# A third raw weight buffer, low parts on VectorE in the gated unit, and token scaling inside the transposing product

## The chip, the core and the metric

The kernel runs on one NeuronCore of a Trainium2 chip. Five engines work side by side, each through its own queue in order: TensorE (PE in the profile: matrix products; PEld is its weight load), VectorE (DVE), ScalarE (ACT), GpSimd (POOL) and SyncE (SP), which here only issues DMAs. GpSimd issues DMAs too, the accumulating ones of this kernel. SBUF is the on-chip memory of 128 partitions; PSUM holds TensorE's results, in 8 banks of 128 x 512 float32. The metric is the device time of one execution in microseconds.

## What is computed

One decoder block, batch 1, 512 tokens of width 1024 with 16 meta tokens put in front (528 in all), float32 throughout:

```python
h = jnp.concatenate([meta, x], axis=1)
n = _rmsnorm(h, g_mix[layer])
proj = n @ w_in[layer]                       # 1024 -> z 1024 | xbc 1536 | dt 16 | u 1024
xbc = jax.nn.silu(_causal_depthwise_conv(proj[..., o_xbc:o_dt], conv_w[layer], conv_b[layer]))
y_ssd = _ssd_mixer(xbc, dt_raw, z, ...)      # Mamba-2, 16 heads of 64, state 128
y_s5 = _s5_mixer(u, ...)                     # 64 groups, complex diagonal scan, then the gated unit
mix = jnp.concatenate([y_ssd, y_s5], axis=-1)
h = h + mix @ w_out[layer]
m = _rmsnorm(h, g_mlp[layer]) @ w_up[layer]
h = h + jnp.square(jax.nn.relu(m)) @ w_down[layer]
return _rmsnorm(h, g_final)[:, N_META:]
```

The gated unit at the end of the S5 branch is `v = gelu(y) @ w_glu + b_glu`, 1024 by 2048, and `v[:, :1024] * sigmoid(v[:, 1024:])`, normed.

## The kernel before

**Split products.** TensorE multiplies in a reduced float32 (F32R), so each operand is split into a high part (a cast) and a low part (what the cast lost), and each product is three: high with high, high with low, low with high. Tokens are kept transposed (width on the partitions), as `xhi` and `xlo`. A weight tile of 128 x 8 x 128 values (512 KB) goes through three rings in the pool `wp`: `load_weight` (L102) loads it into `raw` (2 buffers) from SyncE's queue, and `split_weight` (L108) makes `whi` and `wlo` (3 buffers each). There are two ways for the low part. With `lo_engine=V` ScalarE casts the high part (L116) and VectorE subtracts it from the raw tile (L117). Otherwise ScalarE writes minus the rounded tile into `wlo` (L120), a DMA from GpSimd's queue adds the raw tile to it (L121), and ScalarE casts the high part (L122). The raw buffer is free when its last reader is done, in the second way the DMA. Loads and splits are given a lead (`AHEAD`, 3000 instructions) in the planner's order.

**Order.** The program is written in the order of the block, but a planner, which simulates the engines with its own instruction times, sets the order on each queue: the ready instruction with the highest priority goes next, so that xbc and z tiles fill the gaps of S5, and gated tiles those of the SSD chunks. At run time each queue keeps that order and waits with semaphores.

**Stages, in the order of time.** (1) Norm and transposition: `norm_transpose_split` (L164) for the meta tokens and four tiles of 128 tokens. `rstd_of` (L145) squares on ScalarE (L148) and takes the power on GpSimd (L151); VectorE multiplies the tile by the factor (L166); TensorE transposes it in eight 128 x 128 pieces against `ident` (L170); VectorE multiplies by the gain (L172), ScalarE casts the high part (L175), VectorE subtracts (L176). (2) Eight u tiles (`u_split` L244, `u_half` L249), 24 products each per half of the tokens, copied to `ut` and to DRAM (`Ud`). Tiles 0 and 1 are loaded between the tokens; tile 2 has VectorE's low part, the other seven GpSimd's. GpSimd clears the tables `WB`, `CC`, `Tp` and two `decay` buffers behind the last power (L478 to L480). (3) Eight S5 blocks (`s5_block` L489): small products, VectorE scans over `decay` (L572), round trips through DRAM (`Kd` to `Tp`, `Ud` to `ub`, `Yd`), with 12 xbc and 8 z tiles as filling, all by GpSimd's way. (4) The gated unit (L875 to L898), 16 weight tiles by GpSimd's way, filling the SSD chunks (L724): there `ab`, the decay rows of eight heads, is read from DRAM by SyncE (L749), masked by GpSimd (L752), exponentiated by ScalarE (L756) and multiplied on VectorE (L758). ScalarE's copy `btok` (L798) feeds the state product `pst` (L801). `sg` and `y5` of the gated unit (L882, L886) have two buffers each. (5) The output product (`rows_product` L818): S5 half first (VectorE's low parts), then the SSD half in two column halves, the first of four slabs with GpSimd's low parts (L934), the second with VectorE's. (6) The MLP in four quarters: `up_tile` (L953) and `block_product` (L1050), a seven-product scheme whose sums `S1`, `S2`, `S3` are tiles made by `Sums.new` (L1025).

Of the kernel before, what the change touches and what calls it, by code (L numbers as in the profile page):

```python
# [10 lines left out]
F32 = mybir.dt.float32  # L11
# [3 lines left out]
ALU = mybir.AluOpType  # L15
# [3 lines left out]
P = 128  # L19
SEQ = 512  # L20
# [3 lines left out]
DM = 1024  # L24
# [7 lines left out]
TS5 = 4  # L32
NC5 = L // TS5
# [5 lines left out]
AHEAD = 3000  # L39
# [6 lines left out]
def bc(ap, axis, n):  # L46
    a = ap.unsqueeze(axis)
    shape = list(a.shape)
    shape[axis] = n
    return a.broadcast_to(shape)  # L50
# [3 lines left out]
def hybrid_block_kernel(ctx, tc, x, meta_tokens, g_mix, w_in, conv_w, conv_b, dt_bias, a_log, d_ssd,  # L54
                        g_ssd, lam_re, lam_im, log_step, b_re, b_im, c_re, c_im, d_s5, w_glu, b_glu,
                        g_s5, w_out, g_mlp, w_up, w_down, g_final, out, dbg=None):
    nc = tc.nc
    V, A, G, T = nc.vector, nc.scalar, nc.gpsimd, nc.tensor
# [42 lines left out]

    def load_weight(src, a, b, ahead=AHEAD):  # L102
        with (tc.high_priority(offset=ahead) if ahead else nullcontext()):
            raw = wp.tile([P, a, b], F32, tag="raw", name="raw", bufs=2)
            dma(out=raw, in_=src)
        return raw

    def split_weight(raw, lo_engine=None, ahead=AHEAD, room=None):  # L108
        with (tc.high_priority(offset=ahead) if ahead else nullcontext()):
            if room is None:  # L110
                hi = wp.tile(list(raw.shape), F32R, tag="hi", name="whi", bufs=3)
                lo = wp.tile(list(raw.shape), F32R, tag="lo", name="wlo", bufs=3)
            else:
                hi, lo = room("whi", list(raw.shape)), room("wlo", list(raw.shape))
            if lo_engine is V:
                A.copy(hi, raw)  # L116
                V.tensor_tensor(out=lo, in0=raw, in1=hi.bitcast(F32), op=ALU.subtract)  # L117
            else:

                A.mul(lo, raw, -1.0)  # L120
                G.dma_start(out=lo.bitcast(F32), in_=raw, accum_op=ALU.add)  # L121
                A.copy(hi, raw)  # L122
        return hi, lo
# [4 lines left out]
    def w_cols(w, c0, n=P, lo_engine=None):  # L128
        return split_weight(load_cols(w, c0, n), lo_engine)
# [15 lines left out]
    def rstd_of(src, n, name):  # L145
        junk = scr[:, 3]
        v = mid.tile([P, 1], F32, tag="ssq", name="ssq")
        A.activation(out=junk[:n], in_=src, func=AF.Square, accum_out=v[:n])  # L148
        V.tensor_scalar(out=v[:n], in0=v[:n], scalar1=1.0 / DM, scalar2=EPS, op0=ALU.mult, op1=ALU.add)
        r = mid.tile([P, 1], F32, tag="rstd", name=name)  # L150
        last_pow.append(G.tensor_tensor(out=r[:n], in0=v[:n], in1=mhalf[:n, 0:1], op=ALU.pow))  # L151
        return r
# [9 lines left out]
            V.tensor_tensor(out=xlo[:, 4 * h:4 * h + 4, c0:c0 + n], in0=src_p, in1=hi.bitcast(F32), op=ALU.subtract)  # L162

    def norm_transpose_split(src, n, gcol, xhi, xlo, c0):  # L164
        r = rstd_of(src, n, "rstd")
        last_xn.append(V.tensor_scalar(out=src, in0=src, scalar1=r[:n, 0:1], scalar2=None, op0=ALU.mult))  # L166
        for h in range(2):
            pt = bank("pt")
            for k in range(4):
                T.transpose(pt[:, k * n:(k + 1) * n], src[:, (4 * h + k) * P:(4 * h + k + 1) * P], ident[:n, :n])  # L170
            xg = xgs[:, next(turn) % 3, 0:4 * n].rearrange("p (k n) -> p k n", k=4)
            V.tensor_tensor(out=xg, in0=pt[:, 0:4 * n].rearrange("p (k n) -> p k n", k=4),  # L172
                            in1=bc(gcol[:, 4 * h:4 * h + 4], 2, n), op=ALU.mult)
            hi = xhi[:, 4 * h:4 * h + 4, c0:c0 + n]
            A.copy(hi, xg)  # L175
            V.tensor_tensor(out=xlo[:, 4 * h:4 * h + 4, c0:c0 + n], in0=xg, in1=hi.bitcast(F32), op=ALU.subtract)  # L176

    s5_ctx = tc.tile_pool(name="s5", bufs=1)
    s5 = s5_ctx.__enter__()
    scr = slot("scr", [P, 4, DM])  # L180
    mt = scr[0:NM, 2]
    xgs = scr[:, 0:2].rearrange("p a (h c) -> p (a h) c", h=2)
    turn = itertools.count()
    last_pow, last_xn = [], []
    xt = slot("xt", [P, 4, DM])
    xhi = slot("xhi", [P, KD, L], F32R)
# [56 lines left out]

    def u_split(f):  # L244
        raw = first_raw[f] if f in first_raw else load_cols(w_in[0], O_U + f * P)
        uw[f] = split_weight(raw, V if f == 2 else G, 0 if f < 3 else AHEAD)
        uts[f] = s5.tile([P, TS5, NC5], F32, tag="ut", name="ut", bufs=2)

    def u_half(f, i):  # L249
# [222 lines left out]
    NB = 2  # L472
# [1 line left out]
    CC = [s5.tile([P, 2, 4, 5, 2, 16], F32, name=f"CC{i}") for i in range(NB)]  # L474
    Tp = [s5.tile([P, 4, P], F32, name=f"Tp{i}") for i in range(NB)]

    decay = [s5.tile([P, 4, NC5], F32, name=f"decay{i}") for i in range(NB)]
    with tc.issue_after(last_pow[-1].ins):  # L478
        for t in (WB, *CC, *Tp, *decay):
            G.memset(t, 0.0)  # L480
    Kd = [dr.tile([P, P], F32, name=f"Kd{f}") for f in range(8)]

# [6 lines left out]
    def s5_block(b):  # L489
# [65 lines left out]
        for hf in range(2):  # L555
# [10 lines left out]
            V.tensor_tensor(out=wi[:, jj], in0=px[1], in1=co[:, jj], op=ALU.mult)  # L566
            V.tensor_tensor(out=tw[:, jj], in0=px[0], in1=si[:, jj], op=ALU.mult)
            V.tensor_tensor(out=wi[:, jj], in0=wi[:, jj], in1=tw[:, jj], op=ALU.subtract)
        A.copy(decay[i][:, :, 1:], bc(r4[:, js], 2, NC5 - 1))
        for w in (wr, wi):  # L570
            w = w.rearrange("p j c -> p (j c)")
            V.tensor_tensor_scan(out=w, data0=decay[i].rearrange("p j c -> p (j c)"), data1=w, initial=0.0,  # L572
                                 op0=ALU.mult, op1=ALU.add)
        sr = s5.tile([P, 4, NC5], F32, tag="sr", name="sr", bufs=1)
        si_ = s5.tile([P, 4, NC5], F32, tag="si", name="si", bufs=1)
# [297 lines left out]
    sqa = sd.tile([P, SEQ], F32, tag="sqa", name="sqa", bufs=1)  # L873
    yy = (yghi, yglo)
    for f in range(8):  # L875
        wv = w_cols(w_glu[0], f * P)
        pv = bank("pv")
        mm_cols(pv, wv, yy, P, slice(0, SEQ))
        wg = w_cols(w_glu[0], DM + f * P)
        pg = bank("pg")  # L880
        mm_cols(pg, wg, yy, P, slice(0, SEQ))
        sg = sd.tile([P, SEQ], F32, tag="sg", name="sg")  # L882
        A.activation(out=sg, in_=pg, func=AF.Tanh, scale=0.5, bias=hbg[:, 8 + f:9 + f])
        hv = mid.tile([P, SEQ], F32, tag="acc", name="hv")
        A.activation(out=hv, in_=pv, func=AF.Identity, scale=0.5, bias=hbg[:, f:f + 1])
        y5 = sd.tile([P, P, TS5], F32, tag="y5", name="y5")  # L886
        V.scalar_tensor_tensor(out=y5.rearrange("p c t -> p t c"), in0=sg.rearrange("p (t c) -> p t c", t=TS5),
                               scalar=1.0, in1=hv.rearrange("p (t c) -> p t c", t=TS5), op0=ALU.add, op1=ALU.mult)
        y5f = y5.rearrange("p c t -> p (c t)")
        if f == 0:  # L890
            dump("y50", y5f)
            A.activation(out=sqa, in_=y5f, func=AF.Square)
        else:
            A.activation(out=sg, in_=y5f, func=AF.Square)
            vadd(sqa, sqa, sg)
        A.activation(out=y5hi[:, f], in_=y5f, func=AF.Copy, scale=col("gs5", f))
        V.scalar_tensor_tensor(out=y5lo[:, f], in0=y5f, scalar=col("gs5", f), in1=y5hi[:, f].bitcast(F32),
                               op0=ALU.mult, op1=ALU.subtract)  # L898
# [32 lines left out]
        transpose_split(xs[:, t], P, hhi, hlo, t * P)  # L931

    ylist = [(yhi[:, k], ylo[k // 2][:, k % 2]) for k in range(KD)]
    rows_product(ylist, w_out[0], 0, 4, 0, G, mix_first)  # L934
    spares = [slot2(name, [P, 3, 2, 512], F32R) for name in ("spareh", "sparel")]
    spare = iter([t[:, n] for n in range(3) for t in spares])

# [80 lines left out]
    class Sums:  # L1018
# [4 lines left out]
            self.s = {}  # L1023

        def new(self, m):  # L1025
            self.s[m] = ml.tile([P, 2, HT], F32, tag=m, name=m, bufs=1 if m == "S3" else 2)
            return self.s[m]

        def get(self, m):
# [126 lines left out]
```

## Time and profile before

| | |
|---|---|
| median of 3 runs | 848.06 us (844.64 to 848.61) |
| profiled execution | 852.09 us, of which 850.4 us from its first to its last instruction |
| mean granted TensorE clock | 0.973 |
| weight tiles with GpSimd's low part / VectorE's | 47 / 42 |
| bytes moved by DMA | 116.28 MB, 24.64 MB of it on GpSimd's queue |
| GpSimd's 47 low-part DMAs, median from issue to landing | 5.3 us |

A row of groups gives the line, the engine, the operation, what is written and read, the count, busy us and mean ns, then the idle time before and what ended it. A row of waits gives the waiting engine and line, what it waited for, total us, times and the longest. A row of stages gives the stretch, each engine's busy us with its count, the granted clock, the DMA share and GB/s. A row of the chain of work or of a timeline starts with start and duration in us.

### The profile page before, as it was taken

How to read it: one execution, taken by the hardware profiler on the slowest of the kernel's cores; microseconds unless marked ns; L12 is line 12 of the kernel's file. 1: busy time of each engine (PE TensorE's matmuls, PEld its weight loads, DVE VectorE, ACT ScalarE, POOL GpSimd, SP SyncE). 2: the span in 40 equal slices, each digit the busy share in tenths (PEclk: the TensorE clock that was granted, in tenths of full speed). 3: DMA queues.
4: the chain of work that ended last, by engine and by line, in shares of the span. 5: the costliest groups of instructions: out<-in, count | busy, mean ns of one | idle time of the engine just before them, and what ended most of it. 6: DMA issues, size and time to landing. Idle time of an engine off the chain costs nothing.

```text
span 850.4 us, 11626 instructions
## 1 busy us (share of the span) xinstructions
PE 794.7 (93%) x4351; PEld 669.5 (79%) x4351; DVE 585.0 (69%) x961; ACT 449.8 (53%) x711; POOL 66.9 (8%) x115
## 2 busy tenths in 40 slices
PE   5998799899899599879999999999999999999996
PEld 4898799898787387667888888888888888888875
DVE  6873789989765456556731557688848885887395
ACT  7575589788655646536513344345334533543254
POOL 5110001011000111111001010000000000000001
PEclk9999999999999889998999999999999999999998
DMA  9988665667677588776626636434133423331002
GB/s 220 187 202 187 151 151 121 157 151 175 163 156 200 124 184 187 162 167 153 235 74 151 176 111 208 124 99 149 55 94 105 143 75 94 104 124 49 1 2 99
DMA packets 144865, 116.28 MB, mean 137 GB/s; under 512 B 22092, under 2 KB 122616, under 8 KB 144808
## 3 DMA queue, kind: packets, MB, share of 16 engines
q1 hardware_dynamic: 138040, 90.89, 37.6%
q0 software_dynamic: 6768, 24.64, 15.5%
q8 instruction: 34, 0.56, 0.3%
q14 instruction: 23, 0.19, 0.1%
HBM read 83.93 MB, written 6.95 MB: 107 GB/s over the span
## 4 chain that ended last, share of the span: by engine, by line
PE 66%; DMA 15%; ACT 6%; DVE 4%; issue 4%; SPq 4%; POOL 0%; POOLq 0%; ACTq 0%; DVEq 0%
PE pm L138 21%; PE acc L1067 16%; PE acc L824 8%; DMA wlo<-raw 5%; PE pg L138 4%; DMA ab<-aD 3%; PE pv L138 3%; PE pxb L138 3%; PE acct L824 3%; PE acct L1067 3%; PE pz L138 2%; DMA raw<-in_w_in_dram 2%; DMA Tp<-Kd 1%; ACT wlo L120 1%; DMA Ud<-ut 1%
## 5 line engine op out<-in xcount | busy, mean ns | idle before, releaser
L138 PE MATMUL pm<-hhi,wlo 128*128 128x512 f32 (+1 forms) x272 | 104.1, 383 | 0.0
L138 PE MATMUL pm<-hhi,whi 128*128 128x512 f32 (+1 forms) x272 | 103.5, 382 | 0.0
L138 PE MATMUL pm<-hlo,whi 128*128 128x512 f32 (+1 forms) x272 | 102.6, 378 | 0.0
L117 DVE TENSOR_TENSOR wlo<-raw,whi 128x1024 fp32r<-128x1024 f32 x42 | 51.4, 1223 | 65.7 <-ACT whi L116 65.6
L116 ACT CAST whi<-raw 128x1024 fp32r<-128x1024 f32 x42 | 44.1, 1050 | 92.1 <-PE pm L138 59.8
L122 ACT CAST whi<-raw 128x1024 fp32r<-128x1024 f32 x47 | 49.1, 1044 | 62.6 <-DMA raw<-in_w_in_dram 19.9
L1067 PE MATMUL acc<-bh,al 128*128 128x512 f32 x192 | 75.7, 394 | 0.1
L1067 PE MATMUL acc<-bl,ah 128*128 128x512 f32 x192 | 75.7, 394 | 0.0
L1067 PE MATMUL acc<-bh,ah 128*128 128x512 f32 x192 | 69.9, 394 | 1.4 <-ACT ah L971 1.4
L121 POOL DMA_DIRECT2D wlo<-raw x47 | 40.6, 864 | 304.7 <-ACT wlo L120 135.2
L971 ACT CAST bh<-quad 128x1024 fp32r<-128x1024 f32 x32 | 33.7, 1054 | 49.5 <-PE acc L1067 42.4
L138 PEld LDWEIGHTS pm<-hlo,whi 128*128 128x128 f32 x272 | 51.1, 188 | 11.2
L138 PEld LDWEIGHTS pm<-hhi,wlo 128*128 128x128 f32 x272 | 51.0, 188 | 10.9
L138 PEld LDWEIGHTS pm<-hhi,whi 128*128 128x128 f32 x272 | 50.9, 188 | 10.0
L138 PE MATMUL pxb<-xhi,whi 128*128 128x264 f32 x192 | 56.6, 295 | 0.4 <-ACT xcr L686 0.4
L138 PE MATMUL pxb<-xhi,wlo 128*128 128x264 f32 x192 | 56.5, 294 | 0.0
L138 PE MATMUL pxb<-xlo,whi 128*128 128x264 f32 x192 | 56.2, 293 | 0.0
L966 DVE TENSOR_TENSOR bl<-quad,bh 128x1024 fp32r<-128x1024 f32 x32 | 39.1, 1223 | 18.6 <-ACT bh L971 18.6
L120 ACT ACTIVATE wlo<-raw 128x1024 fp32r<-128x1024 f32 x47 | 49.6, 1056 | 4.1 <-DMA raw<-in_w_glu_dram 3.9
L971 ACT CAST bh<-quads 128x1024 fp32r<-128x1024 f32 x24 | 25.2, 1051 | 41.5 <-PE acc L1067 23.3
L1067 PEld LDWEIGHTS acc<-bh,ah 128*128 128x128 f32 x192 | 36.0, 188 | 9.7 <-ACT ah L971 2.1
L1067 PEld LDWEIGHTS acc<-bh,al 128*128 128x128 f32 x192 | 36.6, 191 | 8.5 <-DVE al L966 0.5
(382 smaller groups left out, 2067.2 us busy)
## 6 DMA issues: line engine op xcount, KB each, us to landing
wlo<-raw POOLq DMA_DIRECT2D x47, 512.0 KB, 5.3
raw<-in_w_up_dram SPq DMA_DIRECT2D x32, 512.0 KB, 4.0
raw<-in_w_in_dram SPq DMA_DIRECT2D x28, 512.0 KB, 4.3
raw<-in_w_glu_dram SPq DMA_DIRECT2D x16, 512.0 KB, 4.5
raw<-in_w_out_dram SPq DMA_DIRECT2D x16, 512.0 KB, 3.4
quad<-in_w_down_dram SPq DMA_DIRECT2D x16, 512.0 KB
quads<-in_w_down_dram SPq DMA_DIRECT2D x16, 512.0 KB, 5.4
ab<-aD SPq DMA_DIRECT2D x8, 512.0 KB, 10.9
```

The source lines that it names most:

```text
L116: A.copy(hi, raw)
L117: V.tensor_tensor(out=lo, in0=raw, in1=hi.bitcast(F32), op=ALU.subtract)
L120: A.mul(lo, raw, -1.0)
L121: G.dma_start(out=lo.bitcast(F32), in_=raw, accum_op=ALU.add)
L122: A.copy(hi, raw)
L138: T.matmul(ps_out, lhsT=w[a][:, k, 0:m], rhs=x[b][:, k, tok], start=(n == 0), stop=(n == len(steps) - 1))
L824: T.matmul(acc[t], lhsT=lhs[2 * sl + k][a][:, t * P:(t + 1) * P], rhs=wt[b][:, k], start=(sl == 0 and k == 0 and n == 0), stop=(sl == n_sl ...
L966: V.tensor_tensor(out=out, in0=a, in1=b, op=ALU.subtract)
L971: A.copy(hi, src)
L1067: T.matmul(banks[bk][s], lhsT=as_[g][x][:, j, s * P:(s + 1) * P], rhs=bs[g][y][:, j], start=(first and g == 0 and j == 0 and i == 0), stop ...
```

## The change

Six edits. `raw` gets a third buffer. The low parts of the 16 gated tiles, of u tile 0 and of the four slabs of L934 move from GpSimd's DMA to VectorE's subtraction: then 26 tiles have GpSimd's low part and 63 VectorE's. The token tile is no longer multiplied by its factor; ScalarE writes the factor on a diagonal (`ident` times the factor, one of three places in the scratch tile), and the transposing product takes that diagonal as its moving operand, so it scales and transposes at once. `decay`, `sg` and `y5` lose their second buffer, and `S3` uses the buffers of `S1`.

```diff
     def load_weight(src, a, b, ahead=AHEAD):
...
-            raw = wp.tile([P, a, b], F32, tag="raw", name="raw", bufs=2)
+            raw = wp.tile([P, a, b], F32, tag="raw", name="raw", bufs=3)
...
     def norm_transpose_split(src, n, gcol, xhi, xlo, c0):
         r = rstd_of(src, n, "rstd")
-        last_xn.append(V.tensor_scalar(out=src, in0=src, scalar1=r[:n, 0:1], scalar2=None, op0=ALU.mult))
+        m = next(turn) % 3
+        diag = scr[:, 1, 640 + m * P:640 + (m + 1) * P]
+        last_xn.append(A.mul(diag[:n, :n], ident[:n, :n], r[:n, 0:1]))
         for h in range(2):
             pt = bank("pt")
             for k in range(4):
-                T.transpose(pt[:, k * n:(k + 1) * n], src[:, (4 * h + k) * P:(4 * h + k + 1) * P], ident[:n, :n])
-            xg = xgs[:, next(turn) % 3, 0:4 * n].rearrange("p (k n) -> p k n", k=4)
+                T.matmul(pt[:, k * n:(k + 1) * n], lhsT=src[:, (4 * h + k) * P:(4 * h + k + 1) * P], rhs=diag[:n, :n])
+            xg = xgs[:, next(xturn) % 3, 0:4 * n].rearrange("p (k n) -> p k n", k=4)
...
-    turn = itertools.count()
+    turn, xturn = itertools.count(), itertools.count()
...
-        uw[f] = split_weight(raw, V if f == 2 else G, 0 if f < 3 else AHEAD)
+        uw[f] = split_weight(raw, V if f in (0, 2) else G, 0 if f < 3 else AHEAD)
...
-    decay = [s5.tile([P, 4, NC5], F32, name=f"decay{i}") for i in range(NB)]
+    decay = s5.tile([P, 4, NC5], F32, name="decay")
     with tc.issue_after(last_pow[-1].ins):
-        for t in (WB, *CC, *Tp, *decay):
+        for t in (WB, *CC, *Tp, decay):
             G.memset(t, 0.0)
...
-        wv = w_cols(w_glu[0], f * P)
+        wv = w_cols(w_glu[0], f * P, lo_engine=V)
...
-        wg = w_cols(w_glu[0], DM + f * P)
+        wg = w_cols(w_glu[0], DM + f * P, lo_engine=V)
...
-        sg = sd.tile([P, SEQ], F32, tag="sg", name="sg")
+        sg = sd.tile([P, SEQ], F32, tag="sg", name="sg", bufs=1)
...
-        y5 = sd.tile([P, P, TS5], F32, tag="y5", name="y5")
+        y5 = sd.tile([P, P, TS5], F32, tag="y5", name="y5", bufs=1)
...
-    rows_product(ylist, w_out[0], 0, 4, 0, G, mix_first)
+    rows_product(ylist, w_out[0], 0, 4, 0, V, mix_first)
...
-            self.s[m] = ml.tile([P, 2, HT], F32, tag=m, name=m, bufs=1 if m == "S3" else 2)
+            self.s[m] = ml.tile([P, 2, HT], F32, tag="S1" if m == "S3" else m, name=m, bufs=2)
```

## What was predicted before the result was known

> **What bounds the kernel now.** I read the busy shares first, then the same figures by stage, then the waits of each stage.
>
> ```profile
> PE 794.7 (93%) x4351; PEld 669.5 (79%) x4351; DVE 585.0 (69%) x961; ACT 449.8 (53%) x711; POOL 66.9 (8%) x115
> ```
>
> ```profile
> core 0: us, PE busy (x) PEld busy (x) DVE busy (x) ACT busy (x) POOL busy (x), PEclk, DMA share, GB/s
> 0.00:30.00 30.00, 17.91 (x103) 15.99 (x104) 21.18 (x42) 18.25 (x36) 11.99 (x51) 0.89 0.98 215
> 30.00:80.00 50.00, 47.32 (x375) 46.70 (x374) 32.72 (x109) 35.50 (x65) 6.10 (x8) 0.97 0.79 186
> 80.00:265.00 185.00, 172.58 (x1308) 157.96 (x1307) 153.61 (x294) 135.18 (x215) 17.00 (x20) 0.98 0.68 155
> 265.00:413.00 148.00, 128.79 (x660) 99.11 (x659) 81.92 (x145) 80.98 (x152) 20.96 (x22) 0.93 0.73 171
> 413.00:825.00 412.00, 412.00 (x1855) 337.60 (x1853) 279.25 (x346) 166.97 (x222) 7.75 (x10) 1.00 0.36 108
> ```
>
> TensorE works 794.7 of 850.4 us, so all there is to win is 56 us of idle time and some lost clock. The stages say where: 12.1 us idle before 30, 2.7 to 80 (the u tiles), 12.4 to 265 (S5 with the xbc and z tiles), 19.2 from 265 to 413 (the gated unit with the SSD chunks), nothing from 413 to 825, where TensorE is busy 412.00 of 412.00 us, and the rest, 9.3, in the tail, which the change doesn't touch. In the gated stage the wait views, of TensorE, SyncE's queue and GpSimd, name the cause:
>
> ```profile
> PE pg L138 <- DMA wlo<-raw: 8.0, 1, 8.0
> PE pst L801 <- ACT btok L798: 5.9, 1, 5.9
> PE pcb L751 <- DVE S L808: 3.6, 1, 3.6
> ```
>
> ```profile
> SPq L105 <- DMA wlo<-raw: 79.9, 12, 12.9
> ```
>
> ```profile
> POOL ab L752 <- DMA ab<-aD: 48.3, 5, 26.0
> ```
>
> Columns of a wait: total us, times, longest. SyncE's queue stood 79.9 of 148 us in front of a weight load whose raw buffer was still being read by the accumulating DMA that makes the low part. The queue runs in order, so the decay rows `ab` for the SSD chunks wait behind such loads. The timelines of SyncE and GpSimd and the chain of work show it:
>
> ```profile
> 357.01 14.12 SPq L105 DMA_DIRECT2D raw<-in_w_glu_dram  x3
> 371.23 3.91 SPq L749 DMA_DIRECT2D ab<-aD  x2
> ```
>
> ```profile
> 292.20 1.10 POOL L752 TENSOR_SCALAR_AFFINE_SELECT ab<-ab 128x1024 f32<-128x1024 f32 x1 [26.03 <-DMA ab<-aD]
> 293.25 0.86 POOL L121 DMA_DIRECT2D wlo<-raw  x1
> ```
>
> ```profile
> 297.82 7.70 PE pg L138 x22
> ...
> 383.99 3.78 PE pst L801 x4
> ```
>
> Three loads took SyncE from 357.01 to 371.13; only then were two `ab` issued, the mask, the exponentials and the copy `btok` came late, and TensorE stood 5.9 us before `pst` (383.99). The other way round, GpSimd waited 26.03 us for `ab` with the DMA of a low part queued behind the mask (293.25): that is the 8.0 us before 297.82.
>
> **The change, part by part.** *Low parts on VectorE in the gated unit (16), the first output slab (4) and u tile 0 (1).* Each removes a ScalarE multiply, a GpSimd DMA and its flight, and adds one VectorE subtraction:
>
> ```profile
> L117 DVE TENSOR_TENSOR wlo<-raw,whi 128x1024 fp32r<-128x1024 f32 x42 | 51.4, 1223 | 65.7 <-ACT whi L116 65.6
> ...
> L120 ACT ACTIVATE wlo<-raw 128x1024 fp32r<-128x1024 f32 x47 | 49.6, 1056 | 4.1 <-DMA raw<-in_w_glu_dram 3.9
> ...
> wlo<-raw POOLq DMA_DIRECT2D x47, 512.0 KB, 5.3
> ```
>
> In the gated stage VectorE gains 16 x 1.22 = 19.6 us and is then busy 81.9 + 19.6 = 101.5 of 148; ScalarE loses 16 x 1.06 = 16.9. From raw to low part was 1.06 + 0.86 + a 5.3 us flight; it becomes 1.22 behind the cast. So the raw buffer is free some 6 us sooner, and nothing of the weights is left on GpSimd's queue there: its masks wait for `ab` alone. *Third raw buffer:* the load after next no longer blocks SyncE. Together they remove what stood before the 8.0 us (the DMA behind the mask), and the blocked `ab` behind the 5.9; the 3.6 goes with them, since VectorE's S update (L808) stood behind a ScalarE square that stood behind `ab`. Lost clock goes too: 22 `pg` in 7.70 us and 4 `pst` in 3.78 us against
>
> ```profile
> 407.50 5.55 PE pg L138 x24
> ...
> 321.76 1.72 PE pst L801 x4
> ```
>
> is 7.70 - 22 x 5.55 / 24 = 2.6 and 2.1 us. In all 17.5 + 4.7 = 22 us; bounds 0 (another wait ends last each time) and 22. I take 18: each wait removed uncovers a smaller one (the late `yf` loads stay, and VectorE now queues 16 more instructions), and 4 us is about one of the three.
>
> *The four subtractions of the output slab, one buffer instead of two for sg, y5 and decay, and S3 in S1's buffers* cost nothing: the first and the last lie in the stretch in which TensorE never idles, sg and y5 are written once in some 18 us (148 / 8) and read by instructions of about 1 us, and decay's copy waits for scans of the block before. What covers them is those gaps; without it each reuse costs about 1 us, 8 us over the eight pairs.
>
> *Scaling inside the transposing product.* The four 128-row VectorE multiplies go, and a 16-row one; ScalarE gets five 128x128 multiplies instead.
>
> ```profile
> PE pt L170 <- DVE xt L166: 5.4, 3, 2.2
> ```
>
> ```profile
> L166 DVE TENSOR_SCALAR xt<-xt,rstd x4: 744/754/5524, 7.8 to 17.4; 128x1024 f32<-128x1024 f32 x4
> ```
>
> ```profile
> L480 POOL MEMSET decay<- x2: 528/528/528, 21.3 to 21.8; 128x528 f32 x2
> L480 POOL MEMSET WB<- x1: 942/942/942, 17.3 to 17.3; 128x1024 f32 x1
> ```
>
> ```profile
> 16.33 0.28 ACT L261 CAST wdt_parts<-scr 128x128 fp32r<-128x128 f32 x1
> ```
>
> These are views of one line (shortest, median and longest ns, first and last start). The fourth multiply, started at 17.4, took 5.52 us where the shortest took 0.74, exactly while GpSimd cleared buffers, from 17.3 to 21.8 + 0.5 = 22.3. With 0.28 us (a 128x128 instruction on ScalarE) in its place, TensorE gets back the 2.2 us of that wait and 0.74 - 0.28 = 0.46 in each of the three other waits for a scaled tile (two of these rows, one of the meta tokens): 3.6 us, plus part of the clock lost in this stage (30 x 0.11 = 3.3 us). Bounds: minus 3.6 - 3.3, and nothing, or worse, if the next VectorE instruction stalls beside the clearing. The Trainium skill, SBUF — State Buffer, section "Who interferes with whom", says that a VectorE instruction in its two-port mode and a GpSimd instruction exclude each other for a whole instruction, and that one with at most one SBUF input outside that mode is not held; the 5.52 beside 0.74 us agrees, no row shows the second half here, and without it 4.8 us of the front would stay.
>
> Against this stands the third buffer: the load for u tile 2 asks for a lead of 3000 instructions and now finds a free buffer at the start, so it can go ahead of the tokens. 512 KB at the measured rate
>
> ```profile
> 5.00:10.00 5.00, 2.40 (x15) 2.30 (x16) 2.85 (x9) 3.69 (x8) 1.36 (x3) 1.00 1.08 356
> ```
>
> is 1.5 us later for every token tile. I take 2.7 us for the front: 3.6 + 0.6 of clock - 1.5. The product itself costs the same as the transposition:
>
> ```profile
> L772 PE MATMUL pyo<-bcr,S 128*128 128x128 f32 x64 | 9.5, 289 | 0.0
> ...
> L733 PE MATMUL ptx<-ident,xcr 128*128 128x128 f32 x32 | 4.6, 289 | 0.0
> ```
>
> The Trainium skill, FP8 and Floating Point Precision, section "TensorE Precision Notes", speaks against it: true FP32 is four passes through the array. The trace differs: FP32 `pst` takes 0.43 us for 512 columns where the one-pass `pg` takes 0.23, under twice as long, and the 289 ns above are equal. By the four passes the sum would be rival (e)'s.
>
> *The u tiles.*
>
> ```profile
> PE pu L138 <- DMA wlo<-raw: 0.6, 1, 0.6
> ```
>
> ```profile
> 65.25 5.88 DMA Ud<-ut
> ```
>
> Of the 2.7 us idle from 30 to 80, 0.6 is a wait for a low part whose raw load had stood behind one of two buffers; it goes. The other 2 us hang on the copy to DRAM of an earlier tile (second row, from the chain of work): ScalarE can't write the next `ut` before it lands; they stay. Taken 0.6, bounds 0 and 2.7. The S5 stage keeps GpSimd's DMAs, and its 12.4 us idle I leave as they are: 0, bounds -5 and +5 for a new order of the filling xbc and z tiles.
>
> **Sum:** 18 + 2.7 + 0.6 = 21.3 us. The profiled execution took 852.09 us (850.4 of span and 1.7 around it), so 830.8; the median of the runs shown is 848.06, 4.0 lower, so I give 848.06 - 21.3 = **826.8**.
>
> **Rivals.** *(a) Only the first gated wait goes* (8.0 + 2.6), because `ab` itself is late (48.3 us of GpSimd's waiting), and the tokens' delay eats the front: 848.06 - 10.6 = 837.5. For it speaks that the planner orders queues by its own times. *(b) Everything goes:* 22, 3.6 + 2.4 at the front without the delay, 2.7 of the u tiles and 6 of S5, half its idle time: 848.06 - 36.7 = 811.4. For it speaks that SyncE's queue is blocked in all stages; against it that S5 keeps GpSimd's DMAs. *(c) Slower: VectorE's queue takes the place of GpSimd's.* A subtraction that waits for its cast stops the SSD work behind it (xdt, the masks' product, S), and TensorE waits for that. Price: VectorE has 148 - 101.5 = 46.5 us idle in the stage, 2.9 us for each of 16 subtractions; beyond it every microsecond counts 16 times. Where VectorE makes low parts now it waited
>
> ```profile
> DVE wlo L117 <- ACT whi L116: 65.6, 24, 11.3
> ```
>
> 65.6 / 24 = 2.7 us each, just below, at most 11.3. At half as much again, 4.1 us, 16 x 4.1 - 46.5 = 19 us are lost, and only 3.3 won ahead of the stage: 864. *(d) The change doesn't do what it says:* the rings of three high and three low parts bind as the raw ring did, or a new plan makes as many holes: 848, within 4. *(e) The scaling product takes four passes against one of a transposition.* 4 `pst` in 1.72 us are 0.43 for 512 columns of FP32, 0.11 for 128; three passes more for 32 of them are 10.3 us in the front: 837.1.
>
> **How the numbers follow.** Forecast 0.50 (its own range 818 to 834), (a) 0.19, (b) 0.12, (e) 0.03, (d) 0.08, (c) 0.08. All but (c) and (d) are faster by over 0.5% (4.2 us, about what a measurement of this kernel can tell from no change): 0.84; within it 0.08; slower 0.08. The range 808 to 844 leaves out (c), (d) and the end of (b), some 0.18.
>
> **What would show it.** Right: no TensorE wait on a low part's landing after 265; SyncE's wait for `wlo` in that stage far below 79.9 us; the stage of 148 us shrunk by 15 to 22; no VectorE instruction over 2 us before 30; no `pu` wait for a low part. Wrong: VectorE's waits for `whi` over 2.9 us each in the gated stage; TensorE waits there for `ab`'s followers as before; the first token tile landing over 2 us later; the stretch from 413 on no longer full.

## Result, and the profile after

The changed kernel takes 821.17 us (median of 4 runs, 819.06 to 822.21) against 848.11 us (844.64 to 848.61): a ratio of 0.9688, 95% interval 0.9656 to 0.972. That is 26.9 us, where 21.3 were forecast. Of the kernels below, one needs a word: three of e13's ten runs were slow (851.42 to 858.00 us) and are left out of its ratio, and its profile is of one of these.

The busy shares of the changed kernel, and its stages, cut where its own stages end (start and end, then busy us and count of PE, PEld, DVE, ACT and POOL, then PEclk, DMA share, GB/s):

```profile
PE 788.0 (96%) x4391; PEld 667.4 (81%) x4391; DVE 601.7 (73%) x977; ACT 431.2 (53%) x695; POOL 48.9 (6%) x93
```

```profile
0.00:30.00 30.00, 23.07 (x164) 22.44 (x165) 14.45 (x32) 19.51 (x38) 10.67 (x49) 1.00 0.90 206
30.00:72.60 42.60, 42.60 (x353) 42.16 (x352) 31.40 (x112) 32.17 (x61) 6.10 (x8) 1.00 0.98 227
72.60:254.50 181.90, 170.82 (x1292) 155.88 (x1291) 155.81 (x298) 135.05 (x217) 15.27 (x18) 0.97 0.66 153
254.50:382.80 128.30, 123.76 (x673) 96.90 (x673) 96.98 (x155) 66.84 (x135) 9.51 (x8) 1.00 0.54 137
382.80:794.30 411.50, 409.84 (x1846) 335.95 (x1845) 285.81 (x355) 166.03 (x224) 4.27 (x6) 1.00 0.33 102
```

The profiled spans are 850.4 and 819.7 us, 30.7 apart (the profile of before was 4.0 above its median). By the start of the last product of each stage, the u tiles end at 72.7 us instead of 80.1 (7.4 saved), S5 with xbc and z takes 181.9 instead of 185.4 (3.5), the gated stage 128.3 instead of 147.4 (19.1), and all that follows 436.8 instead of 437.5 (0.7). The shares also tell in which coin: idle time of TensorE fell from 850.4 - 794.7 = 55.7 us to 819.7 - 788.0 = 31.7. The other 6.7 us are busy time, which a higher clock shortens and the new transposing product lengthens (below). In the gated stage the granted clock rose from 0.93 to 1.00; before 30 us it rose, by the record, from 0.89 to 1.00 (how far the record goes there is said in the last section).

The waits of the gated stage of the changed kernel, TensorE's, SyncE's, GpSimd's and VectorE's:

```profile
PE pcb L754 <- DVE S L811: 3.5, 3, 2.0
PE pst L804 <- ACT btok L801: 0.8, 2, 0.4
```

```profile
SPq L105 <- DVE wlo L117: 67.6, 14, 8.9
```

```profile
POOL ab L755 <- DMA ab<-aD: 106.3, 7, 47.9
DVE wlo L117 <- ACT whi L116: 11.7, 5, 6.0
```

TensorE no longer waits for a low part; its 17.5 us of three waits are 4.3 us in small pieces. SyncE still stands 67.6 us before weight loads, now behind VectorE's subtraction instead of a DMA, and no wait of TensorE's products there is put down to a weight. GpSimd waits longer than before (106.3 us against 48.3), and this costs little, because no weight stands behind its mask any more. It does not cost nothing: in the chain of work all three `pcb` waits, 3.5 us, end a path that starts with a load of `ab` (for the first, the load from 291.68 to 301.31, then mask, exponentials, a cast, a low part and VectorE's sums up to `pcb` at 309.63). The total of a wait is not its price: what is queued behind it is. VectorE's wait for its casts, on which the slower rival hung, is 11.7 us in all, 0.7 for each of 16 subtractions, where 2.9 was the point of decision. One sign of being wrong came, in small: behind 382.8 us TensorE is idle for 411.50 - 409.84 = 1.7 us, where the kernel before keeps it busy throughout; all that follows the gated stage is no longer for it.

### The profile page after: what moved, and what is told of

It reads as the page before. It is cut to its first block, busy times and chain, and to the rows that moved or that the text cites. A ratio compares the mean times of both kernels' runs of the same rounds, so it can differ in the third digit from the quotient of the medians.

```text
span 819.7 us, 11655 instructions
## 1 busy us (share of the span) xinstructions
PE 788.0 (96%) x4391; PEld 667.4 (81%) x4391; DVE 601.7 (73%) x977; ACT 431.2 (53%) x695; POOL 48.9 (6%) x93
## 4 chain that ended last, share of the span: by engine, by line
PE 75%; DVE 9%; DMA 7%; ACT 5%; issue 2%; SPq 1%; POOL 1%; POOLq 0%; ACTq 0%; DVEq 0%
PE pm L138 22%; PE acc L1070 13%; PE acc L827 8%; PE pu L138 6%; PE pz L138 5%; DMA ab<-aD 3%; PE pg L138 3%; PE pxb L138 3%; PE acct L827 3%; PE pv L138 2%; PE acct L1070 2%; PE pyd L771 1%; PE px L564 1%; DMA Tp<-Kd 1%; DMA raw<-in_w_in_dram 1%
## 5 line engine op out<-in xcount | busy, mean ns | idle before, releaser
L117 DVE TENSOR_TENSOR wlo<-raw,whi 128x1024 fp32r<-128x1024 f32 x63 | 77.0, 1222 | 72.8 <-ACT whi L116 71.7
L138 PE MATMUL pxb<-xhi,wlo 128*128 128x264 f32 x192 | 55.7, 290 | 0.0
L1070 PEld LDWEIGHTS acc<-bh,al 128*128 128x128 f32 x192 | 36.5, 190 | 8.3 <-DVE al L969 0.3
L1070 PEld LDWEIGHTS acc<-bl,ah 128*128 128x128 f32 x192 | 36.5, 190 | 8.0
L138 PE MATMUL pu<-xhi,whi 128*128 128x264 f32 x128 | 36.5, 287 | 0.6 <-ACT xhi L178 0.6
```

The costliest lines, as they stand in the source:

```text
L138: T.matmul(ps_out, lhsT=w[a][:, k, 0:m], rhs=x[b][:, k, tok], start=(n == 0), stop=(n == len(steps) - 1))
L1070: T.matmul(banks[bk][s], lhsT=as_[g][x][:, j, s * P:(s + 1) * P], rhs=bs[g][y][:, j], start=(first and g == 0 and j == 0 and i == 0), stop ...
```

## Experiments

Twelve kernels were run in three groups. Each group had its own runs of the kernel before (medians 846.77, 848.31 and 845.86 us), and ratios are against those. The stages are cut at the first and last products, from one profile of each kernel; "S5" includes the xbc and z tiles, and "rest" is all behind the gated stage. The profiles of before, e4 and e13 are of executions 4 to 6 us above their medians.

| kernel | buffers | scaling | u tile 0's low part | gated low parts | u tiles end | S5 | gated | rest | median us | ratio (95%) |
|---|---|---|---|---|---|---|---|---|---|---|
| before | 2 | multiply | GpSimd | GpSimd | 80.1 | 185.4 | 147.4 | 437.5 | 848.11 | 1 |
| changed | 3 | product | VectorE | VectorE | 72.7 | 181.9 | 128.3 | 436.8 | 821.17 | 0.9688 (0.9656 to 0.972) |
| e1 | **2** | product | VectorE | VectorE | 81.4 | 181.3 | 129.0 | 435.4 | 831.26 | 0.9814 (0.978 to 0.9848) |
| e2 | 3 | product | VectorE | **GpSimd** | 72.8 | 182.6 | 135.8 | 439.1 | 831.66 | 0.9818 (0.9781 to 0.9855) |
| e3 | 3 | **multiply** | VectorE | VectorE | 75.9 | 177.3 | 128.4 | 437.2 | 819.73 | 0.9693 (0.9652 to 0.9734) |
| e14 | 3 | product | **GpSimd** | VectorE | 78.8 | 179.8 | 129.2 | 435.4 | 825.09 | 0.9749 (0.9699 to 0.9799) |
| e5 | 2 | multiply | GpSimd | **VectorE** | 78.9 | 182.2 | 129.5 | 436.7 | 829.32 | 0.9779 (0.9745 to 0.9814) |
| e9 | **3** | multiply | GpSimd | GpSimd | 79.8 | 183.7 | 135.6 | 438.1 | 837.85 | 0.9867 (0.9831 to 0.9903) |
| e10 | 2 | **product** | GpSimd | GpSimd | 78.3 | 185.4 | 140.8 | 437.6 | 840.37 | 0.9898 (0.9866 to 0.993) |
| e13 | 2 | multiply | **VectorE** | GpSimd | 80.0 | 185.7 | 146.5 | 437.5 | 845.81 | 0.997 (0.9934 to 1.0007) |
| e4 | 2 | multiply | GpSimd | GpSimd | 80.2 | 185.7 | 146.5 | 437.0 | 846.25 | 0.998 (0.9948 to 1.0012) |

Bold marks the one part that was undone (upper rows) or done alone (lower rows; e4 has only the single-buffer savings).

**e1, e2, e3: one part of the change undone.**

```diff
# e1
-            raw = wp.tile([P, a, b], F32, tag="raw", name="raw", bufs=3)
+            raw = wp.tile([P, a, b], F32, tag="raw", name="raw", bufs=2)
# e2
-        wv = w_cols(w_glu[0], f * P, lo_engine=V)
+        wv = w_cols(w_glu[0], f * P)
-        wg = w_cols(w_glu[0], DM + f * P, lo_engine=V)
+        wg = w_cols(w_glu[0], DM + f * P)
# e3
-        m = next(turn) % 3
-        diag = scr[:, 1, 640 + m * P:640 + (m + 1) * P]
-        last_xn.append(A.mul(diag[:n, :n], ident[:n, :n], r[:n, 0:1]))
+        last_xn.append(V.tensor_scalar(out=src, in0=src, scalar1=r[:n, 0:1], scalar2=None, op0=ALU.mult))
...
-                T.matmul(pt[:, k * n:(k + 1) * n], lhsT=src[:, (4 * h + k) * P:(4 * h + k + 1) * P], rhs=diag[:n, :n])
+                T.transpose(pt[:, k * n:(k + 1) * n], src[:, (4 * h + k) * P:(4 * h + k + 1) * P], ident[:n, :n])
```

> The changed kernel with two raw buffers again, the rest as changed. Theory (both the earlier release by VectorE and the third buffer free SyncE's queue, and the u tiles need the buffer): 826 to 832 us, the u tiles end 3 to 5 us later than 72.7, the gated stage 2 to 5 us longer than 128. Rival (VectorE's low parts alone do it): 821 within 3. Rival (the third buffer does most of it): 838 or more.

> The changed kernel with the 16 gated low parts back on GpSimd's DMA, the third buffer and all else kept. Theory: the gated stage is back near 140 to 147 us and the time 834 to 840. Rival (the third buffer alone frees the queue): the stage stays within 4 us of 128 and the time under 826.

> The changed kernel with VectorE's multiply and the transposition against the identity, all else kept. Theory of the prediction (the 5.5 us multiply beside GpSimd's clearing and three small waits): one multiply of over 5 us again, 2 to 4 us more, 823 to 825. Rival (the products warm the clock where transpositions don't): granted clock in the first 30 us falls from 1.00 to about 0.9, 5 to 7 us more, 826 to 828. Rival (hidden by the u tiles' weights): 821 within 1.5.

**e4: the savings of buffers alone,** all else as before.

```diff
-    decay = [s5.tile([P, 4, NC5], F32, name=f"decay{i}") for i in range(NB)]
+    decay = s5.tile([P, 4, NC5], F32, name="decay")
...
-        sg = sd.tile([P, SEQ], F32, tag="sg", name="sg")
+        sg = sd.tile([P, SEQ], F32, tag="sg", name="sg", bufs=1)
...
-        y5 = sd.tile([P, P, TS5], F32, tag="y5", name="y5")
+        y5 = sd.tile([P, P, TS5], F32, tag="y5", name="y5", bufs=1)
...
-            self.s[m] = ml.tile([P, 2, HT], F32, tag=m, name=m, bufs=1 if m == "S3" else 2)
+            self.s[m] = ml.tile([P, 2, HT], F32, tag="S1" if m == "S3" else m, name=m, bufs=2)
```

> The kernel before with only the buffers taken away (one sg, one y5, one decay, S3 in S1's buffers). Theory: they cost nothing, 848 within 3. Rival: each reuse waits, 8 us over the gated pairs, 856.

What was measured is in the table. Without the third buffer 10 us are lost, and not where the forecast would have them: the gated stage stays at 129.0 us, and the u tiles end 8.7 us later. Without VectorE's gated low parts 10 us are lost as well, 7.5 of them in the gated stage. e1's time came as expected (826 to 832), but from another stage; e2 came to 831.66 us and a gated stage of 135.8, where 834 to 840 and 140 to 147 had been expected. Without the scaling product nothing is lost that can be measured, as e3's last rival had it (821 within 1.5). The sign of e3's other rival came without its price: the granted clock before 30 us fell to 0.89. That does not speak for the kind of instruction, since e1, which has the products, shows 0.89 as well. The savings cost nothing that can be measured.

**e5 and e9: the two remedies of the gated stage, each alone.** Both start from the kernel before; e9 has e4's savings too, which make room for the buffer.

```diff
# e5
-        wv = w_cols(w_glu[0], f * P)
+        wv = w_cols(w_glu[0], f * P, lo_engine=V)
-        wg = w_cols(w_glu[0], DM + f * P)
+        wg = w_cols(w_glu[0], DM + f * P, lo_engine=V)
# e9
-            raw = wp.tile([P, a, b], F32, tag="raw", name="raw", bufs=2)
+            raw = wp.tile([P, a, b], F32, tag="raw", name="raw", bufs=3)
```

> The kernel before with one line pair changed: the low parts of the gated unit's weights on VectorE, two raw buffers, no buffer savings, the multiply as before. Theory A (the gated stage's three waits have one cause, the turn of the raw buffers by the GpSimd queue, and VectorE's parts alone end it; the earlier run with two raw buffers had this stage in 128.8 us): the gated stage shrinks from 147 to about 129 us, the tokens' stage stays, and the time is about 828 us (before less 18 to 19). Rival B (the third buffer and VectorE's parts are each worth the 10 us that was lost when either was taken out, and add up): about 837 us, the gated stage about 137.

> The kernel before with the third raw buffer and the buffer savings that make room for it; low parts of the gated unit and multiply as before. Theory A (two remedies for one stall, not additive; the earlier run with GpSimd's low parts and three buffers had the gated stage in 135.6 us): gated stage about 136 us (11 shorter), u tiles end about 4 us earlier, time about 830 us. Rival B (additive, 10 us each): about 836 us. Rival C (the buffer does nothing in the gated stage while GpSimd's queue carries the low parts): gated stage 147, time about 842 us.

VectorE's low parts alone save 17.9 us of the gated stage, the buffer alone 11.8: the two overlap, and do not add up to 19.1. The kernels of the table repeat this: with GpSimd's parts the stage takes 146.5 to 147.4 us with two buffers (one kernel, e10, stands apart, see below) and 135.6 and 135.8 with three; with VectorE's it takes 128.3 to 129.5 with either. Which wait each removes is in TensorE's waits of the stage, e9's first, then e5's:

```profile
PE pg L138 <- DMA wlo<-raw: 8.4, 2, 7.0
PE pv L138 <- ACT yghi L700: 0.9, 2, 0.7
PE pst L801 <- ACT btok L798: 0.7, 1, 0.7
```

```profile
PE pst L801 <- ACT btok L798: 3.6, 3, 2.2
```

The buffer takes away the waits behind the late `ab` (`pst` 5.9 to 0.7, `pcb` 3.6 to none) and leaves the 8 us behind the low part whose DMA stands behind GpSimd's mask. VectorE's parts take that one away and most of the other two. For the low part that is what the prediction argued. For the buffer the effect is there but the argument isn't borne out: in e9 SyncE still stands 78.8 us before weight loads for low parts (79.9 before), and how the buffer brings `ab` to TensorE in time was not traced. e9's time was foretold too short, 830 against 837.85, because its front did not move (79.8) where 4 us had been expected; the rival's 836 was nearer, but its reason, 10 us from each remedy, does not fit 17.9 and 11.8.

**e10, e13, e14: what the front's gain is made of.** e10 and e13 start from the kernel before, e14 from the changed one.

```diff
# e10
-        last_xn.append(V.tensor_scalar(out=src, in0=src, scalar1=r[:n, 0:1], scalar2=None, op0=ALU.mult))
+        m = next(turn) % 3
+        diag = scr[:, 1, 640 + m * P:640 + (m + 1) * P]
+        last_xn.append(A.mul(diag[:n, :n], ident[:n, :n], r[:n, 0:1]))
...
-                T.transpose(pt[:, k * n:(k + 1) * n], src[:, (4 * h + k) * P:(4 * h + k + 1) * P], ident[:n, :n])
+                T.matmul(pt[:, k * n:(k + 1) * n], lhsT=src[:, (4 * h + k) * P:(4 * h + k + 1) * P], rhs=diag[:n, :n])
# e13
-        uw[f] = split_weight(raw, V if f == 2 else G, 0 if f < 3 else AHEAD)
+        uw[f] = split_weight(raw, V if f in (0, 2) else G, 0 if f < 3 else AHEAD)
# e14
-        uw[f] = split_weight(raw, V if f in (0, 2) else G, 0 if f < 3 else AHEAD)
+        uw[f] = split_weight(raw, V if f == 2 else G, 0 if f < 3 else AHEAD)
```

> The kernel before with the diagonal product in place of VectorE's multiply and the transpositions; two raw buffers and the rest as before. Theory A (on ScalarE the making of the diagonal stands behind a weight's conversion that waits for its load, and with two raw buffers that load waits for a buffer): the third token tile's product waits about 4 us for its diagonal, the u tiles end at 80 to 82 us (no earlier than before), time 846 to 849 us. Rival B (the prediction's own term, 2.7 us less in the front): u tiles end near 77 us, time about 843 us.

> The kernel before with one change: the low part of u tile 0 on VectorE; two raw buffers, multiply and transpositions, and the gated unit as before. Theory A (VectorE's subtraction stands among the multiplies, and the third load still waits for a buffer): u tiles end at 79 to 81 us, the gated stage 147 or a little less, time 845 to 849 us. Rival B (it is worth the same 4 us by itself): u tiles end at 76 us, time 843 to 844 us.

> The changed kernel with the low part of u tile 0 back on GpSimd's accumulating transfer (third buffer, product and everything else stay). In the earlier runs the u tiles end at 79.8 with the third buffer alone, at 75.9 with buffer and VectorE's first low part, at 72.7 with the product too. Theory A (the front's gain needs all three, and the first low part is worth about 3 to 4 us of it): u tiles end at 76 to 77 us, time 823 to 825 us. Rival B (buffer and product carry it, the first low part is worth the 0.6 us or less that the prediction gave it): u tiles end at 73 us, time 821 to 822 us.

Alone, the buffer moves the end of the u tiles by -0.3 us, the product by -1.8, VectorE's first low part by -0.1; together by -7.4. With any one missing the end is later again, by 8.7 us (buffer), 3.2 (product) or 6.1 (low part; 3 to 4 had been expected). Between kernels that share all three parts the end moves by less than 1 us. Each part removed leaves a different wait in one of the in-order queues. In e1, ScalarE's timeline:

```profile
20.48 1.04 ACT L116 CAST whi<-raw 128x1024 fp32r<-128x1024 f32 x1 [4.26 <-DMA raw<-in_w_in_dram]
21.43 0.40 ACT L169 ACTIVATE scr<-ident,rstd 128x128 f32<-128x128 f32 x1
```

With two buffers SyncE issues the load of u tile 2 at 14.47 us, with three at 4.16. So its cast stood 4.26 us at the head of ScalarE's queue, and the diagonal of the last token tile stood behind it. In e14, VectorE's:

```profile
18.12 0.22 DVE L300 COPY lrow<-lsr 32x128 f32<-32x128 f32 x1 [3.87 <-DMA lsr<-in_log_step_dram]
18.26 1.21 DVE L117 TENSOR_TENSOR wlo<-raw,whi 128x1024 fp32r<-128x1024 f32 x1
```

A copy of a small row waited 3.87 us for its load, with the token work behind it; in the changed kernel the two stand the other way round, and by then (15.8 us) the row has landed. In e3 it is the long multiply (below), in e9 the same small row (2.71 us) and then the long multiply. And a hole of 4.3 us costs more than itself. The stages of e14 around its hole (17.10 to 21.38 us), and those of the changed kernel:

```profile
16.00:20.00 4.00, 1.10 (x10) 0.90 (x9) 1.88 (x3) 1.69 (x4) 0.00 (x0) 0.98 0.93 181
20.00:24.00 4.00, 2.62 (x12) 2.58 (x13) 4.00 (x10) 2.15 (x4) 3.18 (x4) 0.50 0.76 74
24.00:28.00 4.00, 4.00 (x25) 3.96 (x25) 3.91 (x7) 1.84 (x3) 1.90 (x4) 0.67 0.88 112
```

```profile
16.00:20.00 4.00, 3.44 (x30) 3.09 (x28) 4.00 (x10) 2.53 (x8) 2.60 (x4) 1.00 0.79 186
20.00:24.00 4.00, 4.00 (x36) 3.99 (x35) 4.00 (x7) 2.24 (x4) 2.49 (x4) 1.00 0.74 71
24.00:28.00 4.00, 4.00 (x36) 3.83 (x35) 0.92 (x3) 0.98 (x4) 0.00 (x0) 1.00 0.85 106
```

After the hole TensorE is granted 0.50 and 0.67 of its clock, which loses 4 x 0.50 + 4 x 0.33 = 3.3 us more, and in 24 to 28 us it finishes 25 instructions instead of 36 though it is busy throughout.

e10 held a surprise: 840.37 us, where 846 to 849 or 843 had been expected. Its u tiles behave nearly as expected (78.3), but its gated stage shrank from 147.4 to 140.8 us with nothing changed there. All five engines have the same order of instructions in that stage as before; ScalarE, VectorE and TensorE differ ahead of it, and by a swap or two at the end. TensorE's three waits there are `pg` 7.5, `pst` 5.3 and `pcb` 1.7 us, 3.0 less in all; of the 6.6 us, 4.0 are idle time and 2.6 busy time, at a clock of 0.96 instead of 0.93. So the stage depends on when things arrive, by some 6 us. This was not followed further, and it is a caution: of one kernel's gain there, some can be had by chance.

**e12: the output slab.** The changed kernel with the low parts of four output tiles back on GpSimd.

```diff
-    rows_product(ylist, w_out[0], 0, 4, 0, V, mix_first)
+    rows_product(ylist, w_out[0], 0, 4, 0, G, mix_first)
```

> The changed kernel with the low parts of the output projection's first slab back on GpSimd. Theory A (that edit costs and brings nothing, the stage behind 383 us is full on TensorE either way): same as the changed kernel, 820 to 822.5 us, and the stretch from the last gated product to the end 437 us. Rival B (the four low parts come late by GpSimd's queue, and the first products of the output wait): a TensorE wait of 1.5 to 5 us between 383 and 400 us, time 823 to 826 us.

820.39 us (816.83 to 822.96), ratio 0.9688 (0.9638 to 0.9739), and the rest 435.7 us: that edit does nothing, as foretold.

**e8 and e11: where the front's gain went next.** In the changed kernel the first S5 product waits for a table that goes through DRAM (`Kd` to `Tp`). TensorE's waits in the changed kernel and in e3 (from 74 to 100 us):

```profile
PE py L588 <- DMA Tp<-Kd: 5.0, 1, 5.0
```

```profile
PE py L586 <- DMA Tp<-Kd: 2.1, 1, 2.1
```

By the traces that product starts at 90.8 us in the changed kernel and at 90.5 in e3. The u tiles end 3.2 us earlier with the scaling product, and the wait is 2.9 us longer: the gain is there, and the next stage eats it. e8 and e11 go at this wait.

```diff
# e8, and e11
+    with tc.high_priority(offset=AHEAD):
     V.tensor_copy(lrow[:, 2].rearrange("j (g p) -> j g p", g=2), bc(lsr, 2, 64))
     pl = bank("pl")
...
     A.copy(lcol, pl[:, 0:96].rearrange("p (a j) -> p a j", a=3))
# e11 alone
+    with tc.high_priority(offset=AHEAD):
     pp = bank("pp")
     T.transpose(pp[:, 0:nrow], prow[:nrow], ident[:nrow, :nrow])
...
     A.copy(pcol, pp[:, 0:nrow + 8])
...
-            dma2(out=Tp[i][96 - 32 * t:P - 32 * t, :, 32 * t:P],
+            (G.dma_start if b == 0 else dma2)(out=Tp[i][96 - 32 * t:P - 32 * t, :, 32 * t:P],
```

> The changed kernel, with the three transpositions of the step columns and the copies around them (lrow, pl, lcol) given the priority that weight loads have, so that they go ahead of u tiles on TensorE. Theory A (the 5.25 us of the first S5 product's wait for its table, at 85.5 us, come from the start of VectorE's table arithmetic at 36.5 us after 11.5 us idle, while it began at 28 before): VectorE's arithmetic starts before 30 us, the wait falls to 1 us or less, time 816 to 818 us. Rival B (the table then waits for something else, or the wait is given back at 163 us): same as the changed kernel within 1 us.

> The changed kernel with the step columns early, as in the earlier run, and now also the parameter columns (pp, pcol) at the priority of weight loads, and block 0's four table reads (Tp) issued by GpSimd instead of SyncE, where they stood behind a weight load that waited for its buffer. In the earlier run the lag product of block 0 was done at 75.5 us, its copy waited until 79.9 for the parameter columns, and the table reads were issued from 86.4 on. Theory A (these two waits make the 5.25 us of wait at 85.5): the lag copy at about 76 us, the table landed by 87 us, the wait under 2 us, time 816 to 818 us. Rival B (VectorE's or ScalarE's order behind it gives the gain back in the S5 blocks): 820 to 822 us, with the first S5 wait gone and others grown.

e8 missed: 820.63 us (819.91 to 821.2), ratio 0.9674 (0.9651 to 0.9698), no different from the changed kernel, and the wait grew to 8.0 us. VectorE's arithmetic did start at 24.6 us instead of 36.5, but the time was handed on to a later wait. SyncE's timeline of e8:

```profile
85.88 0.39 SPq L105 DMA_DIRECT2D raw<-in_w_in_dram  x1
86.37 3.37 SPq L536 DMA_DIRECT2D Tp<-Kd  x4
```

The table reads stood behind a weight load that waited 5.3 us for its buffer. e11 sends them by GpSimd's queue and brings the parameter columns forward: 814.89 us (812.23 to 815.45), ratio 0.962 (0.9576 to 0.9664). On the same chip e12, which is the changed kernel but for an edit without effect, took 820.39, so 5.5 us are gained, and **this version beats both**. Its first table wait, and the S5 stretch of the changed kernel's cut in e11 (4 us of the gated stage are in it):

```profile
PE py L590 <- DMA Tp<-Kd: 3.3, 1, 3.3
```

```profile
72.60:254.50 181.90, 173.23 (x1325) 158.49 (x1324) 156.56 (x297) 134.21 (x213) 17.59 (x22) 0.99 0.69 160
```

The wait is 3.3 us where under 2 were expected, and the copy of the lag table came at 79.2 us, 1.1 earlier than in the changed kernel, not at 76. Nor did the reads go out earlier: GpSimd waited 8.7 us for the write of `Kd` and issued them from 86.7 us on, against 86.4 in e8 and 84.5 in the changed kernel, and the first product starts at 91.2 instead of 90.8. The wait is shorter because TensorE had other work up to 87.9 us instead of 85.8. Cut at its own ends, e11's S5 stage takes 176.9 us (73.6 to 250.5) where the changed kernel's takes 181.9: TensorE is idle 8.6 us instead of 11.1 and busy 168.3 instead of 170.8, at a clock of 0.99 instead of 0.97. So the gain is measured, and its place; which of the edits brings it was not tried, and that the reads' new queue does is not shown.

## Why the prediction was right, and where it was not

**The gated stage was right in place and size, and in cause for the most part.** 18 us were taken and 19.1 came: TensorE's idle time there fell from 147.4 - 128.2 = 19.2 to 128.3 - 123.8 = 4.5, and its busy time by 4.4 us, which is the clock that the prediction had put at 4.7. The waits removed are the three named, and what is left of them, 4.3 us, is about the 4 that the sum kept back. The 8 us before a low part fell to VectorE's parts, as argued. What the sum did not say is that these alone would have brought 17.9 us, most of the other two waits with it. The third buffer is not needed there once they are in (e1: 129.0).

**The front was mis-sized:** 2.7 + 0.6 were taken, 7.4 came. TensorE's idle time up to the end of the u tiles fell by 7.9 us, where the sum had 3.6 - 1.5 + 0.6 = 2.7: the three waits for a scaled tile went whole (5.4 us, where 3.6 were taken from these and the meta tokens' wait), no delay came, and the wait for `ut` (2.0) went too. Four steps failed.

*"- 1.5: the load for u tile 2 goes ahead of the tokens."* It went ahead of the last token tile's load, and no token tile was worked on later. ScalarE's square of the last tile, before and after:

```profile
15.28 1.06 ACT L148 ACTIVATE scr<-xt 128x1024 f32<-128x1024 f32 x1
```

```profile
15.09 1.05 ACT L148 ACTIVATE scr<-xt 128x1024 f32<-128x1024 f32 x1
```

*"+ 0.6 of clock", out of 3.3.* All of it came, by the record: the changed kernel has no hole over 0.7 us between 6.6 and 85 us, and no slow stretch there, while a hole in e14 brought one back.

*"The other 2 us hang on the copy to DRAM of an earlier tile; they stay."* They went. Every kernel with two raw buffers has TensorE's wait for ScalarE's `ut` copy (1.9 to 3.5 us in before, e1, e4, e5, e10, e13), none with three has it (changed, e2, e3, e9, e14). In the kernel before, the DMA of the earlier tile had landed by 71.13 us, and the copy started later, at 72.31: it stands in ScalarE's queue behind the cast and the multiply of a weight whose load came late. TensorE's wait and ScalarE's timeline there:

```profile
PE pu L138 <- ACT ut L252: 2.0, 1, 2.0
```

```profile
70.40 1.05 ACT L122 CAST whi<-raw 128x1024 fp32r<-128x1024 f32 x1 [3.43 <-DMA raw<-in_w_in_dram]
71.35 1.05 ACT L120 ACTIVATE wlo<-raw 128x1024 fp32r<-128x1024 f32 x1
72.31 0.36 ACT L252 COPY ut<-pu 128x264 f32<-128x264 f32 x1
```

That load was issued at 64.78 us, after 6.8 us in which SyncE waited for a low part's DMA to free a raw buffer. So the last part of this wait at least belonged to the raw ring, and it goes with the third buffer: from 30 to 80 us ScalarE's casts wait for weight loads in all six kernels with two buffers (3.8 to 14.5 us), and not at all in those five with three.

*"The product itself costs the same as the transposition."* It costs twice as much. The 32 transposing products of the token tiles are 64 MATMUL records in the changed kernel, and 32 transpositions are 32. One token tile, in the changed kernel and in e3:

```profile
18.45 2.05 PE L173 MATMUL pt<-scr,xt 128*128 128x128 f32 x16
```

```profile
25.38 1.06 PE L171 MATMUL pt<-ident,xt 128*128 128x128 f32 x8 [0.86 <-DVE xt L167]
```

That is 2.05 against 1.06 us for the same eight blocks, 4.0 us for four tiles at this clock. The equal 289 ns that the prediction read are per record, and it did not count records per product; its 0.43 us for `pst` was half a product too. Here the Trainium skill, FP8 and Floating Point Precision, section "TensorE Precision Notes", had it right, and the reading of the trace was wrong: eight products of four passes at a quarter of `pg`'s 0.23 us are 8 x 4 x 0.058 = 1.9 us, near the 2.05. Rival (e) named the mechanism, and at 10.3 us sized it too high, since it compared with a transposition of 0.11 us, which by the same measure is two passes. The 4.0 us do not lengthen the front: up to the end of the u tiles TensorE is busy 65.2 us before and 65.7 after, the clock won back paying for the longer product, while its idle time falls from 14.8 to 6.9. That the two cancel was luck, since the sum had neither.

**The long multiply was right, and worth little by itself.** The fourth multiply, 5.52 us before, takes 4.4 to 5.5 us in every kernel that keeps it, beside GpSimd's clearing; in e9 and in e3,

```profile
23.13 5.04 DVE L166 TENSOR_SCALAR xt<-xt,rstd 128x1024 f32<-128x1024 f32 x1 [0.46 <-POOL rstd L151]
```

```profile
20.86 4.37 DVE L167 TENSOR_SCALAR xt<-xt,rstd 128x1024 f32<-128x1024 f32 x1
```

and in none with the product. What VectorE does beside the clearing in the changed kernel (GpSimd's row, then VectorE's) is not held:

```profile
18.80 2.27 POOL L483 MEMSET CC<- 128x1280 f32 x2
```

```profile
19.23 0.67 DVE L175 TENSOR_TENSOR scr<-pt,gcol 128x512 f32<-128x512 f32 x1
19.84 0.67 DVE L179 TENSOR_TENSOR xlo<-scr,xhi 128x512 fp32r<-128x512 f32 x1
```

This is the half of the rule in the Trainium skill, SBUF — State Buffer, section "Who interferes with whom", that no row of before could show (an instruction with at most one SBUF input is not held), and the trace agrees with it for the instruction whose other input lies in PSUM (`scr<-pt,gcol`). The second, with both inputs in SBUF, is outside that half, and took 0.67 us as well. Yet e3, with the multiply back, is as fast as the changed kernel (819.73): 3.2 us of the front are lost and the wait for the first table is shorter.

**S5 was put at 0 and gave 3.5 in the profiles.** In before and e5, which have the same code up to the gated unit, that stretch takes 185.4 and 182.2 us, so 3.5 is not told apart from nothing.

**The rivals.** (a), (c) and (d) fell: three waits went, VectorE's waits stayed at 0.7 us per subtraction, and the stages shrank. (b) overshot: S5 kept its idle time (11.1 of 12.4 us), as the forecast had it. (e) is answered above. The sum, 21.3, is 5.6 short of the measured 26.9. By the profiles, 30.7 apart, the front is short by 4.1, the gated stage by 1.1, and S5, of which 3.5 can be chance, by 3.5.

## What to carry to other kernels

In a queue that runs in order, ask of each wait what stands behind it: 106 us of GpSimd's waiting cost TensorE under 5 once no weight was behind it, and 4 us of ScalarE's or VectorE's put the end of the u tiles 6 to 9 us later where the tokens were. Several parts may each be worth under 2 us alone and 7 together, when each removes one of the waits that hold the same start; undoing one part at a time and doing one alone then give different answers, and both are needed. What is won early in a stage is kept only if the next thing due is ready: here a table's round trip through DRAM ate part of the front's gain.

## What the runs showed of the hardware that was not expected

A hole in TensorE's work at full clock, 4.28 us in e14 and 4.37 in e1, both before 22 us, is followed by some 7 us at half clock (0.50 and 0.67 over 8 us in e14, 0.56 and 0.59 in e1). The Trainium skill, TensorE: Matmul & The Clock Gate, section "HAM oscillation — how this bites in real kernels", sets the bound at idle gaps of about 3.4 us. These two holes agree with it; others don't. The hole of 2.25 us in the kernel before (20.78 to 23.03 us) and one of 2.06 in e10 (25.20 to 27.26) were followed by a slow stretch as well (0.63 from 22 to 26 us, 0.78 from 26 to 30), and one of 3.60 in e10 (84.41 to 88.01) by none, its products starting 0.12 us apart behind it. The length of one hole does not decide it here.

The granted clock of the views does not show the start. All kernels have 1.00 up to their first slow stretch, but in e9 the u products start 0.22 us apart until 23.9 us and 0.12 apart from then on, and in the changed kernel the records of the transposing product start 0.21 us apart until 13.5 us and 0.11 from then on. So the early part runs at half rate whatever the record says. The step from 0.89 to 1.00 stands, since before and changed reach the full rate at about the same time, by 14.1 and 13.7 us.

The kernel before took 841.94 to 852.69 us in 13 runs of one group, and e10 moved its gated stage by 6.6 us without touching it. Whether the changed kernel varies less (819.06 to 822.21 over 4) isn't shown: e12, which differs by an edit without effect, took 816.83 to 822.96.
